# One more pair by seven products in every down quad of a SwiGLU layer, and split row tiles ahead of two phases

## The chip, the cores and the metric

The kernel runs on one core of a Trainium2 chip. The metric is the device time of one execution in microseconds (us); three runs of the kernel before gave a median of 1873.14 us (1871.94 to 1873.9). Engines are named as the profile names them: PE (TensorE, matmuls), PEld (its weight loads), DVE (VectorE), ACT (ScalarE), POOL (GpSimd), SP (SyncE, which issues the DMAs).

## The reference

One decoder layer on 256 tokens of width 2048, in float32. Only the two feed-forward blocks and what lies next to them matter here:

```python
x = x + 0.5 * swiglu(rms_norm(x, g1), w_gate1, w_up1, w_down1)       # FFN1, inner width 5632
h = rms_norm(x, g2); p = h @ w_in                                    # mixing: one projection in
x = x + concat(diff_attention(q, k, v), conv_group(value, gate)) @ w_out
x = x + cross_attention(rms_norm(x, g3), rms_norm(mem, gm))          # ends with @ w_o
x = x + 0.5 * swiglu(rms_norm(x, g4), w_gate2, w_up2, w_down2)       # FFN2, inner width 5632

def swiglu(h, w_gate, w_up, w_down):
    return (silu(h @ w_gate) * (h @ w_up)) @ w_down
```

## The kernel before

All weights (365 MB) come in once as float32 through DMAs that SP issues. Every product is made of three matmul passes on split operands: a weight tile `raw` is cast by ACT to `wh` (L145), and DVE subtracts, `wl = raw - wh` (L146); the activations are split likewise into a high and a low half (`xh`, `xl` for the normed input, `hth`, `htl` for FFN's inner values). High by high, high by low and low by high are summed in PSUM.

The feed-forward blocks run in *quads* (`quad`, L199): four accumulators `acc00` to `acc11`, two token halves by two 512-column blocks. A quad goes through its *parts*, each a pair of 128-row weight tiles of both column blocks: one buffer `raw` of 128x4x512, filled by two DMAs of 512 KB. There are three such buffers (`RAWS`) and seven pairs `wh`, `wl` of 128x1024 (`SPLITS`). An *ordinary part* takes two splits of 1024 columns (so two casts and two subtractions) and 24 matmuls of 128x512. A *seven part* forms the block product with seven products in place of eight: DVE makes sums of weight tiles (L241 to L244), three splits of 1024 columns and one of 512 are needed, and PE does 21 matmuls. Three of the seven products go straight to accumulators, four to the extra sums `p1`, `q6` and `q57`, which `combine` (L286) puts together behind the last seven part; `middle` then adds them to where they belong. A seven part needs sums of the activations too (`token_sums`, L296).

FFN's inner width is 11 chunks of 512, taken in groups of 4, 4 and 3. For each chunk there is one *up quad* of eight parts (gate and up), of which parts 1, 3 and 5 are sevens (`S_IN`); FFN1's first chunk has none. Behind a group stand two *down quads* (`n0` = 0 and 2, one for each half of the output columns): a *down pair*. Their parts are the row pairs of the group's chunks, eight or six, in the order `ORDER_DOWN`; an even part whose chunk number is under `S_DOWN` is a seven: three of eight, two of six. At a down quad's end DVE adds the four accumulators to the residual `X` (L482), and `middle` (L472) adds the seven parts' sums to it in five operations (L477). Where the same X is normed next, `after_x` (L400) books the transposes of the result with `later`, due after so many parts.

`proj` (L149) is the simpler loop for mixing and cross attention: row pairs, two splits of 1024 columns, 24 matmuls. Phases follow in this order: FFN1 to about 714 us, mixing with `w_in` and `w_out`, cross attention with `w_o`, FFN2 from 1167 us to the end. At a boundary the buffers' pools change.

A scheduler in the framework puts each engine's instructions into one fixed order beforehand; at run time an engine waits in this order for semaphores, and buffers come free as their readers end.

Of the kernel before, what the change touches and what calls it, by code (L numbers as in the profile page):

```python
# [52 lines left out]
def hybrid_layer(ctx, tc, x, head, xT, mem, memT, pos, convw, bvec, w):  # L53
# [95 lines left out]
    def proj(stats, srcs, evac, acc=None):  # L149
# [10 lines left out]
        for k0 in range(0, nk, per):  # L160
# [11 lines left out]
            ending = evac is not None and k0 + per >= nk  # L172
            for tb in range(2):

                for js in ([[j] for j in range(nj)] if ending else [list(range(nj))]):
                    for k in ks:
                        h, l, i, _ = stats[k]
                        hs = h[:, i, tb * P:(tb + 1) * P]
                        ls = l[:, i, tb * P:(tb + 1) * P]
                        for j in js:  # L180
                            T.matmul(acc[tb][j], hs, wt[k, j][0], start=(fresh and k == 0), stop=False)  # L181
                            T.matmul(acc[tb][j], hs, wt[k, j][1], start=False, stop=False)  # L182
                        for j in js:
# [15 lines left out]
    def quad(parts, srcs, middle, evac, first=False):  # L199
# [6 lines left out]
        acc = [[accp.tile([P, 512], F32, tag=f"acc{tb}{j}", name=f"acc{tb}{j}") for j in range(2)]  # L206
               for tb in range(2)]
        begun = set()
        seven = [i for i, p in enumerate(parts) if p()[4]]
        q = None  # L210
        for n, part in enumerate(parts):
# [177 lines left out]
    class LazyStats:  # L389
        def __init__(self, norm):  # L390
            self.norm = norm

        def __len__(self):
            return KD

        def __getitem__(self, k):
            h, l = self.norm.grp[k // 4] if self.norm.grp[k // 4] else (None, None)
# [11 lines left out]
    def ffn(norm, wg, wu, wd, groups, done):  # L409
        with tc.tile_pool(name="wf", bufs=SPLITS, reuse_waits="tile") as wf, \  # L410
# [8 lines left out]
            for gi, ng in enumerate(groups):  # L419
                hts, hsums, hold = {}, {}, {}  # L420
                s_down = S_DOWN[ng]
                for c in range(c0, c0 + ng):
# [3 lines left out]
                    sevens = () if start else S_IN  # L426
# [10 lines left out]
                    def evac(tb, acc, c=c, rest=rest, end=(c == c0 + ng - 1), pairs=(c - c0 < s_down)):  # L437
# [12 lines left out]
                        def turn():  # L450
# [16 lines left out]

                    quad(norm.parts(order, sevens),
                         [wg[:, c * 512:(c + 1) * 512], wu[:, c * 512:(c + 1) * 512]], middle, evac, first=start)
                final = gi == len(groups) - 1  # L470
                for n0 in (0, 2):
                    def middle(q, n0=n0):  # L472
                        p1, vw = combine(q, fp)
                        for tb, j, t, f in ((0, 0, p1, 0.5), (0, 1, vw[:, 0, :], 0.5), (1, 0, vw[:, 1, :], -0.5),
# [4 lines left out]
                    def evac(tb, acc, n0=n0):  # L479
                        for j in range(2):  # L480
# [97 lines left out]
    def constants_b():  # L578
# [64 lines left out]
    ffn(n1, w["ffn1_w_gate"], w["ffn1_w_up"], w["ffn1_w_down"], (4, 4, 3),  # L643
        lambda tb, n: after_x(n2, tb, n))
# [41 lines left out]
    w_in, w_out, w_kv = w["w_in"], w["w_out"], w["xattn_w_kv"]  # L686
# [5 lines left out]
    with tc.tile_pool(name="mix", bufs=1, reuse_waits="tile") as mp:  # L692
# [8 lines left out]
        for c in range(2):  # L701
# [12 lines left out]
            proj(n2.stats(), [wcols(w_in, 8 + c), wcols(w_in, 6 + c)], evac)  # L714
# [264 lines left out]
    with tc.tile_pool(name="xa", bufs=1, reuse_waits="tile") as ap:  # L979
# [77 lines left out]
        def add_x2(n0):  # L1057
# [5 lines left out]
            return evac  # L1063
        for n0 in (0, 2):
            proj(xst, [wcols(w["xattn_w_o"], n0), wcols(w["xattn_w_o"], n0 + 1)], add_x2(n0))
# [8 lines left out]
    ffn(n4, w["ffn2_w_gate"], w["ffn2_w_up"], w["ffn2_w_down"], (4, 4, 3), store)  # L1074
# [41 lines left out]
```

## Time and profile before

| | |
|---|---|
| median of three runs | 1873.14 us (1871.94 to 1873.9) |
| profiled execution | 1874.74 us, its span 1871.8 us |
| TensorE clock granted, mean over the span | 0.998 |
| busy: PE, PEld, DVE, ACT | 1852.2, 1524.5, 1676.7, 1090.6 us |
| weights read | 361.09 MB from HBM |

Busy time is the sum of an engine's instructions; matmuls overlap one another, and the ends of matmuls are modelled, so the distance of two starts tells their pace better than a duration. A view by stretch gives each engine's busy time in a window; a window's length less an engine's busy time is that engine's idle time there. A timeline lists instructions by start; in square brackets stands how long the engine had been idle before one, and whose result ended this.

### The profile page before, as it was taken

To read this page: it belongs to the slowest core of one execution; us is meant where nothing else is said; L and a number is where in the kernel's file an instruction comes from. 1 tells how busy PE (TensorE), PEld (TensorE's weight loads), DVE (VectorE), ACT (ScalarE), POOL (GpSimd) and SP (SyncE) were. 2 spreads that over 40 slices of the span, in tenths; PEclk is the share of its full clock that TensorE was granted. 3 is DMA by queue.
4 is the path that set the end of the run, shared out by engine and by line. 5 is a ranking of instruction groups with operands and counts; after the bars stand their busy time and mean duration, and the time that the engine had idled before them with its cause. 6 is when DMAs were issued, how large, how long until landed. Compare 5 with 4: busy or idle time off the path is not lost.

```text
span 1871.8 us, 23348 instructions
## 1 busy us (share of the span) xinstructions
PE 1852.2 (99%) x8365; PEld 1524.5 (81%) x8365; DVE 1676.7 (90%) x2240; ACT 1090.6 (58%) x1470; POOL 21.7 (1%) x29
## 2 busy tenths in 40 slices
PE   9999999999999999999999999999999999999998
PEld 6878888888888887888778887888888888888887
DVE  7899999999999996799997666999999999999998
ACT  7565555565545665554577656665655556555553
POOL 0000000000000000000011000000000000000000
PEclk9999999999999999999999999999999999999999
DMA  9556556656665546766644751556655666546554
GB/s 336 199 193 203 180 176 214 212 187 200 205 222 181 202 158 209 230 206 198 178 134 129 256 182 57 203 180 215 207 191 197 227 212 203 191 157 225 186 201 153
DMA packets 188756, 364.72 MB, mean 195 GB/s; under 512 B 11616, under 2 KB 12128, under 8 KB 188640
## 3 DMA queue, kind: packets, MB, share of 16 engines
q1 hardware_dynamic: 188640, 363.23, 58.6%
q8 instruction: 65, 1.06, 0.2%
q14 instruction: 51, 0.42, 0.1%
HBM read 361.09 MB, written 2.10 MB: 194 GB/s over the span
## 4 chain that ended last, share of the span: by engine, by line
PE 71%; DVE 19%; DMA 3%; issue 3%; ACT 3%; POOL 0%; SPq 0%; DVEq 0%; ACTq 0%
PE acc L277 13%; PE acc L281 13%; PE acc L279 13%; DVE wl L146 8%; DVE y L917 4%; PE acc L182 4%; PE acc L181 4%; PE acc L184 4%; PE acc L196 3%; PE q L196 3%; PE q L197 3%; PE acc L197 3%; PE q L195 3%; PE acc L195 3%; DMA raw<-ffn_w_up 2%
## 5 line engine op out<-in xcount | busy, mean ns | idle before, releaser
L145 ACT CAST wh<-raw 128x1024 fp32r<-128x1024 f32 (+1 forms) x864 | 838.3, 1001 | 664.2 <-DVE raw L241 267.0
L146 DVE TENSOR_TENSOR wl<-raw,wh 128x1024 fp32r<-128x1024 f32 (+1 forms) x864 | 975.9, 1158 | 139.6 <-ACT wh L145 124.2
L277 PE MATMUL acc<-wh,xh_f 128*128 128x512 f32 x904 | 352.7, 393 | 6.5 <-ACT wh L145 3.6
L279 PE MATMUL acc<-wl,xh_f 128*128 128x512 f32 x904 | 351.6, 391 | 0.0
L281 PE MATMUL acc<-wh,xl_f 128*128 128x512 f32 x904 | 294.4, 390 | 0.0
L277 PEld LDWEIGHTS acc<-wh,xh_f 128*128 128x128 f32 x904 | 169.7, 188 | 45.9 <-ACT wh L145 6.0
L279 PEld LDWEIGHTS acc<-wl,xh_f 128*128 128x128 f32 x904 | 170.1, 188 | 36.5 <-DVE wl L146 2.0
L281 PEld LDWEIGHTS acc<-wh,xl_f 128*128 128x128 f32 x904 | 170.0, 188 | 35.5
L277 PE MATMUL acc<-wh,hth 128*128 128x512 f32 x448 | 174.7, 392 | 0.7 <-DVE vw L442 0.4
L279 PE MATMUL acc<-wl,hth 128*128 128x512 f32 x448 | 174.5, 390 | 0.0
L281 PE MATMUL acc<-wh,htl 128*128 128x512 f32 x448 | 147.9, 390 | 0.0
L181 PE MATMUL acc<-wh,xh_mix 128*128 128x512 f32 x320 | 125.6, 394 | 1.8 <-ACT wh L145 1.8
L182 PE MATMUL acc<-wl,xh_mix 128*128 128x512 f32 x320 | 125.3, 392 | 0.5 <-DVE wl L146 0.5
L241 DVE TENSOR_TENSOR raw<-raw 128x1024 f32<-128x1024 f32 x95 | 115.5, 1216 | 0.0
L196 PE MATMUL q<-wl,sh 128*128 128x512 f32 x285 | 110.9, 389 | 0.0
L197 PE MATMUL q<-wh,sl 128*128 128x512 f32 x285 | 110.9, 389 | 0.0
L195 PE MATMUL q<-wh,sh 128*128 128x512 f32 x285 | 110.9, 389 | 0.0
L184 PE MATMUL acc<-wh,xl_mix 128*128 128x512 f32 x320 | 102.9, 391 | 0.0
L917 DVE SCALAR_TENSOR_TENSOR y<-uT,cw,y 128x256 f32<-128x256 f32 x240 | 100.4, 470 | 0.1
L277 PEld LDWEIGHTS acc<-wh,hth 128*128 128x128 f32 x448 | 84.1, 188 | 19.7 <-DVE vw L442 1.3
L281 PEld LDWEIGHTS acc<-wh,htl 128*128 128x128 f32 x448 | 84.1, 188 | 17.6
L279 PEld LDWEIGHTS acc<-wl,hth 128*128 128x128 f32 x448 | 84.2, 188 | 16.9
(299 smaller groups left out, 2502.7 us busy)
## 6 DMA issues: line engine op xcount, KB each, us to landing
raw<-ffn_w_down SPq DMA_DIRECT2D x176, 512.0 KB, 4.8
raw<-ffn_w_gate SPq DMA_DIRECT2D x175, 512.0 KB, 4.0
raw<-ffn_w_up SPq DMA_DIRECT2D x175, 512.0 KB, 5.2
raw<-w_in SPq DMA_DIRECT2D x80, 512.0 KB, 4.4
raw<-w_out SPq DMA_DIRECT2D x32, 512.0 KB, 4.8
raw<-xattn_w_kv SPq DMA_DIRECT2D x16, 512.0 KB, 3.9
raw<-xattn_w_q SPq DMA_DIRECT2D x8, 512.0 KB, 4.3
raw<-xattn_w_o SPq DMA_DIRECT2D x8, 512.0 KB, 3.8
```

Of the source, the lines that this page charges most:

```text
L145: last[:] = [S.copy(out=wh, in_=raw), V.tensor_tensor(out=wl, in0=raw, in1=wh.bitcast(F32), op=ALU.subtract)]
L146: V.tensor_tensor(out=wl, in0=raw, in1=wh.bitcast(F32), op=ALU.subtract)]
L181: T.matmul(acc[tb][j], hs, wt[k, j][0], start=(fresh and k == 0), stop=False)
L182: T.matmul(acc[tb][j], hs, wt[k, j][1], start=False, stop=False)
L184: T.matmul(acc[tb][j], ls, wt[k, j][0], start=False, stop=(ending and k == nk - 1))
L195: T.matmul(acc, hs, w[0], start=start, stop=False)
L196: T.matmul(acc, hs, w[1], start=False, stop=False)
L197: T.matmul(acc, ls, w[0], start=False, stop=stop)
L277: T.matmul(acc[tb][j], hs, wt[b][j][0], start=f"{tb}{j}" not in begun, stop=False)
L279: T.matmul(acc[tb][j], hs, wt[b][j][1], start=False, stop=False)
L281: T.matmul(acc[tb][j], ls, wt[b][j][0], start=False, stop=(ending and b == 1))
L917: V.scalar_tensor_tensor(out=yc, in0=u[:, j:j + 256], scalar=cw[:, j * 8 + ct:j * 8 + ct + 1], in1=yc, op0=ALU.mult, op1=ALU.add)
```

## The change

1. `S_DOWN` becomes 4 and 3 in place of 3 and 2: every down quad has one more seven part, so twelve in the kernel. Its parts are in a new order, in which the last seven parts stand one behind another (2, 4, 6 after 1, 3, 0, 5; or 0, 2, 4 after 1, 3). The last chunk of a group now needs token sums as well.
2. In the down pairs but those that end a block, `middle` only forms `ys`, and four additions to X (five before) stand behind the accumulators' own.
3. A new class `Lead`: the first row pair of mixing's `w_in` (columns 8 and 6) is loaded and split in FFN1's tiles, at the start of the ending part of its last down quad, and its 24 matmuls come straight behind that quad. FFN2's first gate and up row pair is treated so behind cross attention's last `proj`.
4. FFN2's first quad has sevens at 1 and 5 (before 1, 3 and 5) and another order of parts; part 0 is the lead. Some transposes of normed X are due one part later.

```diff
-ORDER_1 = (0, 2, 1, 4, 3, 6, 5, 7)
+S_1, ORDER_1 = (1, 5), (0, 2, 3, 1, 4, 5, 6, 7)
-S_DOWN = {4: 3, 3: 2}
-ORDER_DOWN = {4: (1, 3, 0, 5, 2, 6, 4, 7), 3: (1, 3, 0, 4, 2, 5)}
+S_DOWN = {4: 4, 3: 3}
+ORDER_DOWN = {4: (1, 3, 0, 5, 2, 4, 6, 7), 3: (1, 3, 0, 2, 4, 5)}
...
+    class Lead:
+        def __init__(self, stats, srcs):
+            self.stats, self.srcs = stats, srcs
+
+        def split(self, tiles):
+            self.w = []
+            for src, (raw, wh, wl) in zip(self.srcs, tiles):
+                nc.sync.dma_start(out=raw, in_=rows_pair(src, 0))
+                split(raw, wh, wl)
+                self.w.append((wh, wl))
+
+        def multiply(self):
+            acc = [[accp.tile([P, 512], F32, tag=f"acc{tb}{j}", name=f"acc{tb}{j}") for j in range(2)]
+                   for tb in range(2)]
+            for tb in range(2):
+                for k in range(2):
+                    h, l, i, _ = self.stats[k]
+                    hs, ls = [t[:, i, tb * P:(tb + 1) * P] for t in (h, l)]
+                    for j in range(2):
+                        wh, wl = [t[:, k, :] for t in self.w[j]]
+                        T.matmul(acc[tb][j], hs, wh, start=(k == 0), stop=False)
+                        T.matmul(acc[tb][j], hs, wl, start=False, stop=False)
+                    for j in range(2):
+                        T.matmul(acc[tb][j], ls, self.w[j][0][:, k, :], start=False, stop=False)
+            step()
+            return acc
...
-            later((1, 2, 2, 3)[n], lambda: norm.turn(n))
+            later(((1, 2, 3, 3) if norm.wanted else (1, 2, 3, 4) if norm is n2 else (1, 2, 2, 3))[n],
+                  lambda: norm.turn(n))
...
-                    sevens = () if start else S_IN
+                    sevens = () if start else S_1 if c == 0 else S_IN
...
                         p1, vw = combine(q, fp)
+                        if not final:
+                            y = fp.tile([P, 512], F32, tag="y", name="ys", bufs=1)
+                            V.tensor_tensor(out=y, in0=vw[:, 0, :], in1=q["q57"][:, 1, :], op=ALU.add)
+                            rest[:] = [(0, 0, p1, 0.5), (0, 1, vw[:, 0, :], 0.5), (1, 0, vw[:, 1, :], -0.5),
+                                       (1, 1, y, 0.5)]
+                            return
...
                             if final:
                                 done(tb, n0 + j)
+                        if tb:
+                            for b, j, t, f in rest:
+                                xt = X[b][n0 + j]
+                                V.scalar_tensor_tensor(out=xt, in0=t, scalar=f, in1=xt, op0=ALU.mult, op1=ALU.add)
...
+                    def ahead():
+                        raw = ph["raw"].tile([P, 4, 512], F32, tag="raw", name="raw")
+                        follow.split([(raw[:, 2 * j:2 * j + 2, :], *split_tiles()) for j in range(2)])
+
+                    leads = final and n0 == 2 and follow
+                    quad(parts, [wd[:, n * 512:(n + 1) * 512] for n in (n0, n0 + 1)], middle, evac,
+                         ahead=ahead if leads else None)
+                    if leads:
+                        return follow.multiply()
...
         for n0 in (0, 2):
-            proj(xst, [wcols(w["xattn_w_o"], n0), wcols(w["xattn_w_o"], n0 + 1)], add_x2(n0))
+            proj(xst, [wcols(w["xattn_w_o"], n0), wcols(w["xattn_w_o"], n0 + 1)], add_x2(n0),
+                 ahead=n0 == 2 and (lambda: lead.split([weight_tiles() for _ in range(2)])))
+        open_acc = lead.multiply()
```

What the scheduler makes of it, first on DVE where FFN1's first down pair goes from its first to its second quad. The numbers behind names are buffers; `wl_2056` to `wl_2093` are the second quad's first two parts, `acc00_1710` is the first quad's accumulator. Before:

```order
L146 TENSOR_TENSOR wl_2056<-raw_2054,wh_2055 128x1024
L146 TENSOR_TENSOR wl_2058<-raw_2054,wh_2057 128x1024
L477 SCALAR_TENSOR_TENSOR x00_73<-p1s_2000,x00_73 128x512
L146 TENSOR_TENSOR wl_2091<-raw_2089,wh_2090 128x1024
L291 TENSOR_TENSOR us_2002<-q6_1821,p1s_2000 128x512
L146 TENSOR_TENSOR wl_2093<-raw_2089,wh_2092 128x1024
L293 TENSOR_TENSOR vw_2004<-q57_1822,us_2002 128x1024
L482 SCALAR_TENSOR_TENSOR x00_73<-acc00_1710,x00_73 128x512
L477 SCALAR_TENSOR_TENSOR x01_74<-vw_2004,x01_74 128x512
L477 SCALAR_TENSOR_TENSOR x10_77<-vw_2004,x10_77 128x512
L477 SCALAR_TENSOR_TENSOR x11_78<-vw_2004,x11_78 128x512
L482 SCALAR_TENSOR_TENSOR x01_74<-acc01_1711,x01_74 128x512
```

The same place after; `wl_2077` and `wl_2079` are the second quad's first part:

```order
L146 TENSOR_TENSOR wl_2077<-raw_2075,wh_2076 128x1024
L328 TENSOR_TENSOR vw_2024<-q57_1834,us_2022 128x1024
L534 SCALAR_TENSOR_TENSOR x00_73<-acc00_1710,x00_73 128x512
L522 TENSOR_TENSOR ys_2026<-vw_2024,q57_1834 128x512
L534 SCALAR_TENSOR_TENSOR x01_74<-acc01_1711,x01_74 128x512
L534 SCALAR_TENSOR_TENSOR x10_77<-acc10_1712,x10_77 128x512
L534 SCALAR_TENSOR_TENSOR x11_78<-acc11_1713,x11_78 128x512
L541 SCALAR_TENSOR_TENSOR x00_73<-p1s_2020,x00_73 128x512
L541 SCALAR_TENSOR_TENSOR x01_74<-vw_2024,x01_74 128x512
L541 SCALAR_TENSOR_TENSOR x10_77<-vw_2024,x10_77 128x512
L541 SCALAR_TENSOR_TENSOR x11_78<-ys_2026,x11_78 128x512
L146 TENSOR_TENSOR wl_2079<-raw_2075,wh_2078 128x1024
```

Four splits of the second quad stood ahead of the accumulators' updates; now one does, and the second comes behind nine operations on ys and X.

On PE at the same place, after, from the seventh matmul of the second quad's first part on:

```order
L312 MATMUL acc00_2071<-wh_2078,hth_143 128x512
L312 MATMUL acc01_2072<-wh_2078,hth_143 128x512
L312 MATMUL acc10_2073<-wh_2076,hth_143 128x512
L314 MATMUL acc10_2073<-wl_2077,hth_143 128x512
L312 MATMUL acc11_2074<-wh_2076,hth_143 128x512
L314 MATMUL acc11_2074<-wl_2077,hth_143 128x512
L316 MATMUL acc10_2073<-wh_2076,htl_144 128x512
L316 MATMUL acc11_2074<-wh_2076,htl_144 128x512
L312 MATMUL acc10_2073<-wh_2078,hth_143 128x512
L312 MATMUL acc11_2074<-wh_2078,hth_143 128x512
L228 MATMUL p1_2167<-wh_2148,hth_143 128x512
L314 MATMUL acc00_2071<-wl_2079,hth_143 128x512
```

With the six before these rows, 17 matmuls stand ahead of the first that reads `wl_2079`; before, the fifth matmul of the quad read the second split (`wl_2058`).

On DVE at the end of FFN1's last down quad, after (`wl_6109` and `wl_6111` are the lead's, of mixing's first row pair; `x02_75` to `x13_80` are the X tiles that the quad ends in):

```order
L326 TENSOR_TENSOR us_6087<-q6_5976,p1s_6085 128x512
L146 TENSOR_TENSOR wl_6109<-raw_6107,wh_6108 128x1024
L328 TENSOR_TENSOR vw_6089<-q57_5977,us_6087 128x1024
L146 TENSOR_TENSOR wl_6111<-raw_6107,wh_6110 128x1024
L529 SCALAR_TENSOR_TENSOR x03_76<-vw_6089,x03_76 128x512
L529 SCALAR_TENSOR_TENSOR x12_79<-vw_6089,x12_79 128x512
L529 SCALAR_TENSOR_TENSOR x13_80<-vw_6089,x13_80 128x512
L534 SCALAR_TENSOR_TENSOR x02_75<-acc00_5859,x02_75 128x512
```

The lead's two splits, which before came behind the phase's end, stand ahead of the four accumulators' updates.

## Rows read from the trace of the kernel before

**Rows 1.** The page's first part: busy time, share of span, instructions.

```profile
PE 1852.2 (99%) x8365; PEld 1524.5 (81%) x8365; DVE 1676.7 (90%) x2240; ACT 1090.6 (58%) x1470; POOL 21.7 (1%) x29
```

**Rows 2.** By stretch: start:end, length, busy (x instructions), clock, DMA share, GB/s.

```profile
core 0: us, PE busy (x) PEld busy (x) DVE busy (x) ACT busy (x) POOL busy (x), PEclk, DMA share, GB/s
193.40:271.70 78.30, 77.59 (x342) 63.91 (x342) 71.87 (x79) 39.03 (x42) 0.00 (x0) 1.00 0.62 202
447.00:524.30 77.30, 77.30 (x342) 63.88 (x341) 71.01 (x78) 38.74 (x41) 0.00 (x0) 1.00 0.62 204
1347.00:1426.60 79.60, 79.60 (x352) 65.61 (x351) 74.09 (x81) 41.60 (x45) 0.00 (x0) 1.00 0.59 198
1600.00:1679.50 79.50, 79.50 (x352) 65.67 (x351) 73.20 (x81) 40.52 (x44) 0.00 (x0) 1.00 0.61 199
657.60:715.00 57.40, 56.82 (x263) 46.95 (x262) 51.68 (x64) 30.96 (x46) 0.33 (x2) 1.00 0.44 141
1812.80:1868.20 55.40, 54.06 (x238) 44.22 (x237) 48.81 (x56) 23.58 (x25) 0.00 (x0) 1.00 0.48 161
268.30:437.50 169.20, 168.49 (x756) 139.46 (x755) 160.23 (x184) 99.08 (x114) 0.00 (x0) 1.00 0.61 205
713.50:718.50 5.00, 2.05 (x12) 1.09 (x10) 3.65 (x8) 4.53 (x11) 0.70 (x1) 0.94 0.95 314
718.50:722.50 4.00, 4.00 (x12) 3.20 (x13) 4.00 (x6) 2.98 (x5) 0.00 (x0) 0.64 0.60 156
```

**Rows 3.** Groups by line and shape, DVE: busy us, mean ns, idle before.

```profile
L146 DVE TENSOR_TENSOR wl<-raw,wh 128x1024 fp32r<-128x1024 f32 x765 | 914.1, 1219 | 138.0 <-ACT wh L145 122.8
L146 DVE TENSOR_TENSOR wl<-raw,wh 128x512 fp32r<-128x512 f32 x99 | 67.6, 683 | 1.6 <-ACT wh L145 1.4
L243 DVE TENSOR_TENSOR raw<-raw 128x512 f32<-128x512 f32 x95 | 65.5, 690 | 2.7
L306 DVE TENSOR_TENSOR sl<-sraw,sh 128x512 fp32r<-128x512 f32 x22 | 15.0, 684 | 2.1 <-ACT sh L305 1.8
```

**Rows 4.** Timeline of PE in a down quad: start, duration (us); parts' first matmuls.

```profile
196.16 0.39 PE L195 MATMUL acc<-wh,hth 128*128 128x512 f32 x1
...
200.92 0.39 PE L277 MATMUL acc<-wh,hth 128*128 128x512 f32 x1
...
206.36 0.39 PE L195 MATMUL acc<-wh,hth 128*128 128x512 f32 x1
```

**Rows 5.** Timeline of DVE and PE behind the first down pair.

```profile
274.29 2.50 DVE L146 TENSOR_TENSOR wl<-raw,wh 128x1024 fp32r<-128x1024 f32 x2
274.74 0.39 PE L195 MATMUL acc<-wh,xh_f 128*128 128x512 f32 x1
...
280.72 1.22 DVE L241 TENSOR_TENSOR raw<-raw 128x1024 f32<-128x1024 f32 x1
...
283.31 6.51 DVE L146 TENSOR_TENSOR wl<-raw,wh 128x1024 fp32r<-128x1024 f32 x6
289.74 1.22 DVE L241 TENSOR_TENSOR raw<-raw 128x1024 f32<-128x1024 f32 x1
```

**Rows 6.** Timeline of DVE: token sums of a chunk.

```profile
183.32 0.28 DVE L299 TENSOR_TENSOR sraw<-hold 128x128 f32<-128x128 f32 x1
183.52 0.28 DVE L300 TENSOR_TENSOR sraw<-hold 128x128 f32<-128x128 f32 x1
```

**Rows 7.** Timeline at the end of FFN1 and the start of mixing.

```profile
713.76 1.27 DVE L482 SCALAR_TENSOR_TENSOR x<-acc,x 128x512 f32<-128x512 f32 x2
...
717.22 0.73 PE L181 MATMUL acc<-wh,xh_mix 128*128 128x512 f32 x2 [1.85 <-ACT wh L145]
...
724.50 0.62 PE L184 MATMUL acc<-wh,xl_mix 128*128 128x512 f32 x2
```

**Rows 8.** Timeline of PE: FFN2's first matmuls, and its fourth up quad's.

```profile
1168.02 1.21 PE L277 MATMUL acc<-wh,xh_f 128*128 128x512 f32 x4 [1.07 <-ACT wh L145]
...
1297.67 0.50 PE L277 MATMUL acc<-wh,xh_f 128*128 128x512 f32 x1 [0.98 <-DVE vw L442]
```

**Rows 9.** Timeline: DVE's last two updates of X.

```profile
1866.92 1.27 DVE L482 SCALAR_TENSOR_TENSOR x<-acc,x 128x512 f32<-128x512 f32 x2
```

More of the change, by code (lines that the diff above doesn't have):

```diff
@@ L146, in split, with proj @@
                    V.tensor_tensor(out=wl, in0=raw, in1=wh.bitcast(F32), op=ALU.subtract)]
-    def proj(stats, srcs, evac, acc=None):
+    def proj(stats, srcs, evac, acc=None, ahead=None):
         nj = len(srcs)
@@ L172, in proj @@
             ending = evac is not None and k0 + per >= nk
+            if ending and ahead:
+                ahead()
             for tb in range(2):
@@ L197, in passes, with quad @@
         T.matmul(acc, ls, w[0], start=False, stop=stop)
[L199 to L208, printed above, removed]
+    def quad(parts, srcs, middle, evac, first=False, acc=None, ahead=None):
+        begun = {"00", "01", "10", "11"} if acc else set()
+        acc = acc or [[accp.tile([P, 512], F32, tag=f"acc{tb}{j}", name=f"acc{tb}{j}") for j in range(2)]
+                      for tb in range(2)]
         seven = [i for i, p in enumerate(parts) if p()[4]]
@@ L270, in quad @@
                 ending = n == len(parts) - 1
+                if ending and ahead:
+                    ahead()
                 wt = [[ev0, ev1], [od0, od1]]
@@ L389, in hybrid_layer, with __init__, after @@
     class LazyStats:
-        def __init__(self, norm):
-            self.norm = norm
+        def __init__(self, norm, first=0):
+            self.norm, self.first = norm, first
+        def after(self, k):
+            return LazyStats(self.norm, k)
         def __len__(self):
-            return KD
+            return KD - self.first
         def __getitem__(self, k):
+            k += self.first
             h, l = self.norm.grp[k // 4] if self.norm.grp[k // 4] else (None, None)
@@ L642, in hybrid_layer @@
     n2 = Norm(G_MIX, "mix")
-    ffn(n1, w["ffn1_w_gate"], w["ffn1_w_up"], w["ffn1_w_down"], (4, 4, 3),
-        lambda tb, n: after_x(n2, tb, n))
+    w_in = w["w_in"]
+    open_acc = ffn(n1, w["ffn1_w_gate"], w["ffn1_w_up"], w["ffn1_w_down"], (4, 4, 3),
+                   lambda tb, n: after_x(n2, tb, n),
+                   follow=Lead(n2.stats(), [w_in[:, c * 512:(c + 1) * 512] for c in (8, 6)]))
     mids = ctx.enter_context(ExitStack())
@@ L713, in evac @@
                 later(2, turn)
-            proj(n2.stats(), [wcols(w_in, 8 + c), wcols(w_in, 6 + c)], evac)
+            ks = n2.stats()
+            if c == 0:
+                proj(ks.after(2), [wcols(w_in, 8), wcols(w_in, 6)], evac, acc=open_acc)
+            else:
+                proj(ks, [wcols(w_in, 8 + c), wcols(w_in, 6 + c)], evac)
         later(5, lambda: behind_last(lambda: preload(AF.Exp)))
```

21 lines of the change are left out of this document (13 added, 8 removed).

## The prediction

> **What bounds the kernel now.** I read the page's first part, then one view of busy time by stretch, then timelines of single places. PE is busy 99% of the span, DVE 90% [rows 1]. The shares hide stages, so the stretches matter: four down pairs behind groups of four chunks (start and end of each: 193.4 to 271.7, 447.0 to 524.3, 1347.0 to 1426.6, 1600.0 to 1679.5), two behind groups of three (657.6 to 715.0, 1812.8 to 1868.2) and the four up quads of FFN1's second group (268.3 to 437.5) [rows 2]. The reader is to see two things. PE has almost no gap in a down pair (77.59 of 78.30, 77.30 of 77.30), so PE sets the pace today. And DVE has little left: idle is length less busy, 6.4, 6.3, 5.5 and 6.3 us in the four large pairs, 5.7 and 6.6 us in the small ones. In the up quads it is 9.0 of 169.2 us. So a change that takes work from PE and gives it to DVE is decided by DVE's idle time, pair by pair.
>
> **What one more seven costs and saves.** On PE a seven part takes 200.92 − 196.16 = 4.76 us and an ordinary part 206.36 − 200.92 = 5.44 us [rows 4]: 21 and 24 matmuls at 0.2267 us, so 0.68 us less for each converted part.
>
> On DVE the starts of two like adds at 280.72 and 289.74 stand 9.02 us apart, with one seven and one ordinary part between [rows 5]. The six splits there (five full, one half) take 6.51 us; the half is 0.68 alone [rows 3], so a full one comes every (6.51 − 0.68)/5 = 1.17 us. An ordinary part is two of them, 2.33; the seven is 9.02 − 2.33 = 6.69. Converting costs DVE 4.36 us. To it come token sums: a group's last chunk, which had none, now needs them. Their small subtractions start 0.20 apart [rows 6], four of them and the 0.68 us subtraction of the casts' copies [rows 3] make 1.48. A pair of down quads gets 2 × 4.36 + 1.48 = 10.2 us of DVE work and loses 1.36 us of PE work. ACT gets three full casts and some copies more, beside 39 us busy of 78 [rows 2]: nothing. DMA carries the same bytes at a share of 0.62 or less in these stretches: nothing.
>
> Here a rule of the Trainium skill can be weighed. The trace shows starts of full splits 1.17 us apart though each lasts 1.219 us [rows 3, 5]. "VectorE: DVE Perf Modes", section "The DRAIN you can't avoid", says that the next operation does not start until the pipe is empty. By that, every operation would cost its whole duration: a conversion 6.94 − 2.44 = 4.50, twelve of them 1.7 us more than in my sum. The trace does not agree for this stream, and I keep 4.36.
>
> **The large pairs.** All of a pair's idle DVE time can at best be used, so DVE arrives late by 10.2 less the idle time: 3.8, 3.9, 4.7, 3.9 us. Against it stands a slack: behind a pair, the first seven part of the next up quad starts on PE at 274.74 and needs its third split after nine matmuls, at 274.74 + 2.04 = 276.78. That split starts at 274.29 and is ready at 274.29 + 1.22 = 275.51 [rows 5], 1.27 us early. I take the same for the other three. PE waits for what is over: 2.5 + 2.6 + 3.4 + 2.6 = **+11.1 us**. PE's saved 1.36 us per pair is not to be taken off again: a PE that has less to do waits longer for the same split. Nothing is carried from one pair into the next, since in an up quad PE takes 10.20 us for a seven and an ordinary part and DVE 9.02, so DVE regains its lead, and each pair pays anew. Where the waits stand the order tells: seven parts 2, 4 and 6 now follow one another at the end of a down quad, and each takes DVE 6.69 against PE's 4.76. The seven pairs of split buffers hold three and a half ordinary parts, so the stock runs out there. At the join of the two quads PE has 17 matmuls (3.85 us) before the first one that needs the second split of the new quad, which DVE now does behind nine operations on X and ys; before, two full parts were split by then. Deferring the four X additions is worth nothing by itself (same operations, behind the accumulators' updates); if it freed the accumulators earlier, PE's gap there is 0.7 us per pair at most (78.30 − 77.59).
>
> Bounds for these four pairs: if none of the idle time were usable they would cost 4 × (10.2 − 1.27) = 36 us; if all lateness sank into the buffers, PE's four times 1.36 would come back, −5.4 us. I stay with +11.1, since DVE's waits for casts in the trace are short and its idle time otherwise comes from full buffers.
>
> **FFN1's last pair and the start of mixing.** Before, DVE's last two updates of X end at 713.76 + 1.27 = 715.03, PE then waits 1.85 us for a cast, and the first 24 matmuls of mixing end at 724.50 + 0.62 = 725.1 [rows 7]. In 713.5 to 722.5 PE loses 5.0 − 2.05 = 2.95 us idle and, at a granted clock of 0.64 for 4.0 us, 1.4 us more [rows 2]. The lead row removes the wait: its two loads go out on SP behind the last down part's instead of behind the phase, its casts on ACT and its two splits on DVE stand ahead of the updates. But those updates are late now: by 10.2 − 5.7 = 4.5 us and the two splits' 2.3, so they end at 721.8. Updates come 0.6 apart (two take 1.27), so the first of four accumulators is free at 721.8 − 1.8 = 720.0; the 24 lead matmuls find the next ones free in time and end at 725.4, and the eight transposes, which stood ahead of them (at most 2.05 − 0.73 = 1.3 us, since the two matmuls at 717.22 lie in that stretch too; I take 0.9), follow: 726.3 against 725.1, **+1.2 us**. Bounds: −3.4 if DVE is not late (the 4.4 us lost fall to 1.0), +4 if the clock falls as before and the next row pair is late too.
>
> **FFN2's start.** The wait of 1.07 us for the first cast goes, since the lead covers it. That of 0.98 us for vw at the start of the fourth up quad, where DVE is still behind from the phase's start, goes too [rows 8]: the first quad has one seven less, 4.36 us less for DVE, and two ordinary parts stand behind its last seven. For PE the missing seven is +0.68. **−1.4 us**; between −2.5 and +0.7.
>
> **FFN2's last pair.** It ends in DVE's updates of X, the last two at 1866.92 [rows 9], and nothing gives slack behind it: 10.2 − 6.6 = **+3.6 us**; between −1.4 and +6.
>
> **Sum.** 11.1 + 1.2 − 1.4 + 3.6 = +14.5. The profiled execution took 1874.74 us (span 1871.8), so 1889.2; the runs' median of 1873.14 is 1.6 lower, so **1888 us**.
>
> **Rivals.** *PE keeps the pace* (faster). The buffers and better order absorb everything: that happens where DVE's arrears at the end of a pair stay under the 1.27 us of slack. For it speaks PE's 99%, and that DVE is 195 us idle over the whole span [rows 1]; against it, that this idle time lies mostly elsewhere and only 5.5 to 6.6 us of it in each pair. Price: eleven net sevens −7.5, boundary −3.4, FFN2's start −2.1 (the waits alone; its seven is in the eleven), together −13.0: 1860 us.
> *Half is absorbed.* DVE gets about half of the lateness back from waits that I did not resolve, for instance of the deferred X additions: between the two, 1874 us, no change.
> *Worse* (slower still). A quarter of DVE's 36.8 us of idle time in the six pairs cannot be used, because it is a wait for a cast: ACT's wh ends most of the idle before the full splits (122.8 of 138.0 us [rows 3]). That is +9.2, and if conversions cost 4.50, +1.7: 1899 us. It decides from the point where the longer runs of sevens make ACT's casts and DVE's splits wait for each other in the seven buffers.
> That the change does not do what it says is no rival: the order shows twelve more seven parts and both lead rows.
>
> **How the numbers follow.** My forecast (own range 1881 to 1895) 0.55; PE keeps the pace 0.19; half 0.14; worse 0.12. About 0.2%, 3.7 us, is what a measurement of this kernel can tell from no change. Faster by more: 0.19 and a third of the half case, 0.24. Same: 0.08, from the half case. Slower: 0.68. The range 1866 to 1898 holds my case, the half case, half of the worse and a sixth of the fast one, about 0.8.
>
> **What would show it.** After the change PE must show gaps that end on DVE's wl: at the start of the second down quad, at the third split of a seven in the run 2, 4, 6, and in the first seven behind a pair, 2.5 to 3.4 us in each large pair; DVE's idle time in the pairs must fall to about 1 us. If PE shows no such gaps and DVE still idles 3 us or more in a pair, the fast rival is right and the step from lateness to waiting is wrong. If DVE idles and PE waits, ACT or the buffers are the cause. At mixing's start I expect no wait for a cast but one for the accumulator, released by an X update; at 1168 no gap.

## Result and the profile after

The changed kernel took 1896.55 us (median of four runs, 1894.89 to 1900.49) against 1872.56 us for the kernel before: a ratio of 1.013, 95% interval 1.0113 to 1.0148. That is 24.0 us slower, where 15 were forecast: 1896.55 us lies just above the forecast's own range (1881 to 1895) and inside the wide one (1866 to 1898). The profiled execution took 1900.49 us, the longest of the four, span 1898.7 us, 26.9 us more than the span before; the stretches below account for these 26.9. Busy times, where [rows 1] stood:

```profile
PE 1855.8 (98%) x8332; PEld 1517.9 (80%) x8332; DVE 1729.3 (91%) x2325; ACT 1110.8 (59%) x1510; POOL 20.4 (1%) x29
```

DVE has 52.6 us more work and PE 33 matmuls fewer. PE's busy time rose all the same. It was not taken apart, but matmuls behind a wait are shown longer (0.50 us where 0.39 is usual, in the rows below), and so are those at half the clock. Where time went is seen from the starts of each stage's first matmul on PE. The third column is the changed kernel with the old table of sevens (experiment 1). All in us:

| stretch | before | after | old sevens |
|---|---|---|---|
| start to the first down pair | 183.55 | 184.74 | 181.62 |
| FFN1, first large pair and the up quads behind | 254.39 | 258.03 | 253.56 |
| FFN1, second | 210.25 | 214.44 | 210.12 |
| FFN1's last pair, mixing, to `w_o` | 492.27 | 498.95 | 487.47 |
| `w_o` and FFN2's first up quads | 199.33 | 196.63 | 196.63 |
| FFN2, first large pair and the up quads behind | 253.05 | 257.05 | 252.49 |
| FFN2, second | 210.25 | 214.82 | 210.12 |
| FFN2's last pair to the end | 68.75 | 74.07 | 68.67 |

The first stretch varied between 181.2 and 184.7 us among the kernels run here and is left out of the reasoning: it took 181.7 us or less where the granted clock held, and 182.9 or more where it fell to 0.50 for 3.41 us near 15 us, as in both kernels' profiled executions. The large pairs gave +3.6, +4.2, +4.0 and +4.6, 16.4 together; FFN1's last pair with mixing +6.7, FFN2's start −2.7, FFN2's end +5.3.

The view by stretch, of the same places as [rows 2] (down pairs without their first two parts, then the four up quads, then FFN1's end):

```profile
core 0: us, PE busy (x) PEld busy (x) DVE busy (x) ACT busy (x) POOL busy (x), PEclk, DMA share, GB/s
194.60:274.40 79.80, 78.03 (x340) 63.31 (x340) 77.53 (x91) 41.75 (x49) 0.00 (x0) 1.00 0.56 185
452.60:530.60 78.00, 76.37 (x334) 62.10 (x333) 75.62 (x88) 41.22 (x47) 0.00 (x0) 1.00 0.58 188
1360.00:1439.60 79.60, 77.67 (x340) 63.20 (x339) 76.99 (x89) 43.53 (x51) 0.00 (x0) 1.00 0.57 185
1616.00:1698.50 82.50, 80.72 (x353) 65.48 (x352) 79.67 (x92) 44.56 (x52) 0.00 (x0) 1.00 0.55 179
666.50:730.40 63.90, 58.13 (x254) 45.43 (x252) 61.84 (x78) 35.84 (x52) 0.33 (x2) 1.00 0.44 140
1834.50:1894.50 60.00, 55.50 (x232) 44.05 (x230) 57.31 (x70) 26.56 (x31) 0.00 (x0) 0.97 0.45 146
271.00:442.50 171.50, 169.34 (x756) 139.58 (x756) 163.74 (x188) 99.54 (x116) 0.00 (x0) 1.00 0.62 209
...
728.90:739.45 10.55, 8.32 (x35) 6.53 (x33) 7.56 (x13) 4.94 (x11) 0.70 (x1) 0.84 0.54 175
```

DVE's idle time in the pairs fell from 5.5 to 6.6 us to 2.3, 2.4, 2.6, 2.8, 2.1 and 2.7: not to about 1. PE now has gaps of 1.6 to 5.8 us in each, where it had 1.3 or less. In FFN2's last pair the clock's mean is 0.97. There, behind waits of 0.47, 0.69 and 0.92 us at the join of the two quads, the granted clock fell to 0.50, that is to 1.2 GHz, for 3.41 us; before, it was 1.00 in this pair:

```profile
1861.90:1865.30 3.40, 3.40 (x10) 2.63 (x9) 3.40 (x4) 0.00 (x0) 0.00 (x0) 0.50 0.65 187
```

PE's waits, by what they wait for (us in total, times, longest), the first of the list after:

```profile
PE acc L228 <- ACT wh L145: 10.1, 12, 1.0
PE acc L314 <- DVE wl L146: 4.8, 5, 1.1
PE p L228 <- ACT wh L145: 4.5, 5, 1.1
```

L228 is the first pass of each of a seven part's products. Behind FFN1's first down pair and in it, timeline of PE; then of DVE in the run of sevens 2, 4, 6 of its first quad; then ACT's casts that end three of these waits:

```profile
232.81 0.50 PE L228 MATMUL p<-wh,hth 128*128 128x512 f32 x1 [1.07 <-ACT wh L145]
...
262.94 0.50 PE L228 MATMUL acc<-wh,hth 128*128 128x512 f32 x1 [0.59 <-ACT wh L145]
...
276.17 0.73 PE L314 MATMUL acc<-wl,xh_f 128*128 128x512 f32 x2 [1.12 <-DVE wl L146]
281.65 0.50 PE L228 MATMUL acc<-wh,xh_f 128*128 128x512 f32 x1 [0.95 <-ACT wh L145]
```

```profile
210.99 0.68 DVE L277 TENSOR_TENSOR raw<-raw 128x512 f32<-128x512 f32 x1
212.86 2.96 DVE L146 TENSOR_TENSOR wl<-raw,wh 128x1024 fp32r<-128x1024 f32 x3 [1.20 <-ACT wh L145]
215.75 1.22 DVE L274 TENSOR_TENSOR raw<-raw 128x1024 f32<-128x1024 f32 x1
```

```profile
211.78 2.52 ACT L145 CAST wh<-raw 128x1024 fp32r<-128x1024 f32 x3 [2.02 <-DVE raw L277]
...
231.19 1.56 ACT L145 CAST wh<-raw 128x1024 fp32r<-128x1024 f32 x2 [2.72 <-DMA raw<-ffn_w_down]
...
280.55 2.00 ACT L145 CAST wh<-raw 128x1024 fp32r<-128x1024 f32 x2 [0.40 <-DVE raw L277]
```

Three of PE's four waits are at places named beforehand: the join of the two down quads (232.81), the third seven of the run in the second quad (262.94) and the first seven behind the pair (281.65); the one at the first part behind the pair (276.17) was not named. Only that one ends on DVE's `wl`, as forecast of all of them; the others end on a cast. One step back it is DVE again: at 281.65 the cast is of a tile that DVE had only just summed (L277). At this join the cast is of an unsummed tile, behind a wait for its load (231.19). But DVE's split for the matmul behind ended within 0.3 us of that cast, here and at the joins of the other three large pairs, so either would have held PE.

DVE's one large idle stretch, 1.20 us at 212.86, stands inside the run, ahead of part 4's last split, with PE on time. The cast that it waits for was not held by a full buffer: ACT itself had waited, for 2.02 us, for the sum that DVE had just ended at 210.99 + 0.68. DVE sums, ACT casts the sum, DVE splits it, and DVE's fixed order puts nothing between. Each of the six down pairs has one such wait, of 1.17 to 1.20 us.

At the two boundaries and the end, where [rows 7 to 9] stood:

```profile
731.52 0.47 PE L216 MATMUL acc<-wh,xh_mix 128*128 128x512 f32 x1 [2.23 <-DVE x L534]
...
1181.59 0.39 PE L216 MATMUL acc<-wh,xh_f 128*128 128x512 f32 x1
...
1893.78 1.28 DVE L534 SCALAR_TENSOR_TENSOR x<-acc,x 128x512 f32<-128x512 f32 x2
```

Mixing's first matmul no longer waits for a cast but for an X update on DVE, 2.23 us; FFN2's first comes 0.23 us behind the one before it, without a wait.

### The profile page after: what moved, and what is told of

It is laid out like the page before. It is cut to its first block, busy times and chain, and to the rows that moved or that the text cites. A ratio compares the mean times of both kernels' runs of the same rounds, so it can differ in the third digit from the quotient of the medians.

```text
span 1898.7 us, 23374 instructions
## 1 busy us (share of the span) xinstructions
PE 1855.8 (98%) x8332; PEld 1517.9 (80%) x8332; DVE 1729.3 (91%) x2325; ACT 1110.8 (59%) x1510; POOL 20.4 (1%) x29
## 4 chain that ended last, share of the span: by engine, by line
PE 57%; DVE 27%; DMA 6%; issue 5%; ACT 4%; SPq 0%; POOL 0%; ACTq 0%; DVEq 0%
DVE wl L146 11%; PE acc L316 9%; PE acc L314 9%; PE acc L312 9%; DVE y L987 4%; PE acc L183 4%; PE acc L186 4%; PE acc L184 4%; ACT wh L145 3%; DMA raw<-ffn_w_down 2%; DVE raw L274 2%; PE acc L228 2%; PE q L229 2%; PE q L230 2%; PE acc L229 2%
## 5 line engine op out<-in xcount | busy, mean ns | idle before, releaser
L145 ACT CAST wh<-raw 128x1024 fp32r<-128x1024 f32 (+1 forms) x886 | 851.7, 997 | 658.8 <-DVE raw L274 270.8
L146 DVE TENSOR_TENSOR wl<-raw,wh 128x1024 fp32r<-128x1024 f32 (+1 forms) x886 | 996.0, 1154 | 119.4 <-ACT wh L145 105.7
L312 PE MATMUL acc<-wh,hth 128*128 128x512 f32 x352 | 135.1, 395 | 3.4 <-DVE x L534 1.4
L314 PE MATMUL acc<-wl,hth 128*128 128x512 f32 x352 | 135.3, 393 | 0.4 <-DVE wl L146 0.4
L274 DVE TENSOR_TENSOR raw<-raw 128x1024 f32<-128x1024 f32 x106 | 129.2, 1219 | 0.1
L228 PE MATMUL q<-wh,sh 128*128 128x512 f32 x318 | 124.7, 392 | 1.3 <-ACT wh L145 0.8
L229 PE MATMUL q<-wl,sh 128*128 128x512 f32 x318 | 124.1, 390 | 0.1
L316 PE MATMUL acc<-wh,htl 128*128 128x512 f32 x352 | 116.4, 392 | 0.0
L312 PEld LDWEIGHTS acc<-wh,hth 128*128 128x128 f32 x352 | 66.3, 189 | 19.7 <-DVE x L534 2.9
L314 PEld LDWEIGHTS acc<-wl,hth 128*128 128x128 f32 x352 | 66.4, 189 | 16.2 <-DVE wl L146 2.6
L316 PEld LDWEIGHTS acc<-wh,htl 128*128 128x128 f32 x352 | 66.4, 189 | 13.7
```

Of the source, the lines that this page charges most:

```text
L145: last[:] = [S.copy(out=wh, in_=raw), V.tensor_tensor(out=wl, in0=raw, in1=wh.bitcast(F32), op=ALU.subtract)]
L146: V.tensor_tensor(out=wl, in0=raw, in1=wh.bitcast(F32), op=ALU.subtract)]
L228: T.matmul(acc, hs, w[0], start=start, stop=False)
L229: T.matmul(acc, hs, w[1], start=False, stop=False)
L274: V.tensor_tensor(out=raw[:, 1:3, :], in0=raw[:, 1:3, :], in1=raw[:, 2:4, :], op=ALU.add)
L312: T.matmul(acc[tb][j], hs, wt[b][j][0], start=f"{tb}{j}" not in begun, stop=False)
```

## Experiments

Times are medians; ratios are against the kernel before on the same chip.

**1. The old sevens, all else changed.**

```diff
-S_DOWN = {4: 4, 3: 3}
-ORDER_DOWN = {4: (1, 3, 0, 5, 2, 4, 6, 7), 3: (1, 3, 0, 2, 4, 5)}
+S_DOWN = {4: 3, 3: 2}
+ORDER_DOWN = {4: (1, 3, 0, 5, 2, 6, 4, 7), 3: (1, 3, 0, 4, 2, 5)}
```

> The changed kernel with the old table of sevens (three of eight, two of six, old order); lead rows, deferred additions and FFN2's first quad stay as changed. Theory (DVE arrears in the down pairs, 26.9 us of span lost there less what the leads give): the loss goes and the leads' gain stays, 2.7 us at FFN2's start and about 1 at mixing's: 1868 to 1870 us. Rival (the leads or the deferred additions cost time themselves): 1873 us or more.

1864.1 us, ratio 0.9958 (0.9943 to 0.9972), and once more, with more rounds:

> The changed kernel with the old table of sevens once more, for comparison on the same chip and with more rounds: 1863 to 1866 us by its first runs.

1864.6 us, ratio 0.9957 (0.9944 to 0.9969). So the sevens cost 32 us, and the rest of the change gives 8, more than the theory's 3 to 4. By the table, 4.8 of these come from FFN1's end and mixing's start and 2.7 from FFN2's start. Some 1.7 of the 4.8 are the clock: before, it was at 0.50 for 3.41 us from 717.93 on; with the old sevens it was 1.00 from 711.50 to 723.50 (second run). With DVE on time the lead runs straight behind the last down part, 0.22 us after its last matmul (second run):

```profile
711.46 0.39 PE L316 MATMUL acc<-wh,htl 128*128 128x512 f32 x1
711.68 0.39 PE L216 MATMUL acc<-wh,xh_mix 128*128 128x512 f32 x1
```

This version beats both kernels and is the best of those tried.

**2. The sevens alone, on the kernel before.**

```diff
-S_DOWN = {4: 3, 3: 2}
-ORDER_DOWN = {4: (1, 3, 0, 5, 2, 6, 4, 7), 3: (1, 3, 0, 4, 2, 5)}
+S_DOWN = {4: 4, 3: 3}
+ORDER_DOWN = {4: (1, 3, 0, 5, 2, 4, 6, 7), 3: (1, 3, 0, 2, 4, 5)}
...
-                                                                  a == 0 and i // 2 < s_down and hsums[c])
+                                                                  a == 0 and i // 2 < s_down and hsums.get(c, True))
```

> The kernel before with only the new table of sevens (one more in each down quad, new order); no lead, no deferral, old first quad of FFN2. Theory (DVE arrears): all of the loss is here, 1896.5 plus the leads' gain of about 3.5: 1899 to 1902 us. Rival (a good part of the loss comes from the lead's two splits ahead of the X updates at FFN1's end, where 6.5 us were lost): 1890 us or less.

1906.5 us, ratio 1.018 (1.0163 to 1.0197): 34 us for the sevens alone. The rival falls. The size was missed here (over the theory's 1902) and in experiment 1 (under its 1868), since the rest of the change gives 8 to 10 us, not 3.5. Of the 10, some 5 are the clock: from the first down pair to 1895 us it was at 0.50 for 17.1 us in this kernel's profiled execution and for 6.8 us in the changed kernel's.

**3. Two ways to take about 5 us of DVE work from each pair.** First the added seven's three sums, in its own chain:

```diff
-                V.tensor_tensor(out=raw[:, 1:3, :], in0=raw[:, 1:3, :], in1=raw[:, 2:4, :], op=ALU.add)
...
-                V.tensor_tensor(out=raw[:, 3, :], in0=raw[:, 3, :], in1=raw[:, 1, :], op=ALU.add)
-                V.tensor_tensor(out=raw[:, 0, :], in0=raw[:, 0, :], in1=raw[:, 3, :], op=ALU.add)
+                if n not in bare:
+                    V.tensor_tensor(out=raw[:, 1:3, :], in0=raw[:, 1:3, :], in1=raw[:, 2:4, :], op=ALU.add)
+                    V.tensor_tensor(out=raw[:, 3, :], in0=raw[:, 3, :], in1=raw[:, 1, :], op=ALU.add)
+                    V.tensor_tensor(out=raw[:, 0, :], in0=raw[:, 0, :], in1=raw[:, 3, :], op=ALU.add)
...
+                         ahead=ahead if leads else None, bare=(ORDER_DOWN[ng].index(2 * s_down - 2),))
```

> The changed kernel without the three sums of weight tiles in the one added seven of each down quad (its products then take unsummed tiles: that part of the result is left out). DVE has 2.58 us less per down quad, 5.2 per pair; PE's and ACT's work is the same. Theory (DVE arrears): 10.2 - 5.2 = 5.0 us added per pair, under the idle time of 5.5 to 6.6 that there was, so arrears all but vanish: 1860 to 1865 us. Rival (the casts or PE's own order set the end): 1890 us or more.

1866.5 us, ratio 0.9968 (0.9957 to 0.9979), just over the theory's 1865. Then additions to X, which no product of the pair waits for:

```diff
+                            if tb == 0 and j == 0:
...
-                            for b, j, t, f in rest:
+                            for b, j, t, f in ():
```

> The changed kernel with the four deferred additions of the sevens' sums to X left out in each down quad (in a block's last pair four of five; that part of the result is left out). DVE has 2.4 us less per quad, 4.8 per pair, and none of it in a seven's own chain of sum, cast, product. Theory (DVE's total work in the pair decides): the same recovery as without the sums but for 0.4 us a pair, 1862 to 1867 us. Rival (the chain sum - cast - product in the run of three sevens decides, where PE waits for ACT's wh): little change, 1890 us or more.

1865.2 us, ratio 0.9962 (0.9947 to 0.9977). Both recover 30 us, the one inside the chain of sum, cast and product and the other outside it, about as much as they take from DVE (six pairs of 5.2 and 4.8 us). So it is the amount of DVE's work that costs PE its time, not that chain: in the second the waits of 1.2 us for the cast of a sum still stand (1.19 us at 209.30), and PE does not feel them. There, the first pair (181.18 to 265.29) and the up quads behind:

```profile
181.18:265.29 84.11, 83.60 (x370) 68.19 (x369) 81.96 (x98) 47.98 (x57) 0.00 (x0) 1.00 0.54 180
265.29:434.15 168.86, 168.86 (x758) 139.80 (x756) 161.41 (x184) 99.28 (x115) 0.00 (x0) 1.00 0.63 212
```

With the same sevens PE loses nothing in the up quads (168.86 of 168.86; after the change 169.34 of 171.50).

**4. The order of parts, and the stock of splits.** The same work with the sevens spread:

```diff
-ORDER_DOWN = {4: (1, 3, 0, 5, 2, 4, 6, 7), 3: (1, 3, 0, 2, 4, 5)}
+ORDER_DOWN = {4: (1, 0, 3, 2, 5, 4, 6, 7), 3: (1, 0, 3, 2, 4, 5)}
```

> The changed kernel with the down parts in another order: sevens spread among the ordinary parts, 1, 0, 3, 2, 5, 4, 6, 7 (groups of four) and 1, 0, 3, 2, 4, 5 (groups of three); the same parts, sums and products. In the changed kernel's first pair DVE idles 1.19 us once ahead of the run 2, 4, 6, with all split buffers full, and 0.12 us in each seven; so theory (idle time early in a quad can't be banked beyond the stock): spreading makes some 1 us per down quad usable, 1884 to 1892 us. Rival (only DVE's total in the pair counts): 1895 to 1899 us.

1889.5 us, ratio 1.0098 (1.0081 to 1.0115): 7 us less, the theory's number but not for its reason. The wait of 1.2 us, which it expected to become usable, still stands in each of the six pairs, and it was no wait for split buffers (above). In the first:

```profile
200.32 2.36 DVE L146 TENSOR_TENSOR wl<-raw,wh 128x1024 fp32r<-128x1024 f32 x2 [1.18 <-ACT wh L145]
```

By the stretches 4.4 us of the gain lie in the large pairs and 2.1 in FFN2's last pair, where the granted clock did not fall here. Why the order helps stays open. And with a smaller stock:

```diff
-RAWS, SPLITS, H_BUFS = 3, 7, 4
+RAWS, SPLITS, H_BUFS = 3, 6, 4
```

> The changed kernel with six pairs of split buffers in place of seven. Theory (a seven needs four of them, and what DVE can do ahead of a run of sevens is limited by this stock): one full split less ahead, 1.17 us, in each of 22 quads at most and in each of 12 down quads at least: 1908 to 1922 us. Rival (DVE's total decides and the stock does not): 1895 to 1900 us.

1903.2 us, ratio 1.0165 (1.0151 to 1.0179): 6.7 us more than with seven, under the theory's 1908 and over the rival's 1900, so neither number held. Of the excess 2.7 us stand in `w_o` and FFN2's first up quads, and 0.1 to 1.5 us in each down pair but FFN1's last, which with mixing is 0.4 us shorter. Order and stock each matter, by about 7 us with the same work.

**5. The deferral.**

```diff
-                        if not final:
+                        if False:
```

> The changed kernel with the sevens' sums added to X at once in every down quad, as before the change (five additions instead of ys and four behind the accumulators). The same number of DVE operations. Theory (DVE's total decides, the deferral is worth nothing by itself): 1894 to 1899 us. Rival (deferral frees the accumulators or p1 for PE earlier and was worth a part of the 10 us by which the changed kernel beats the one with the sevens alone): 1900 to 1904 us.

1899.5 us, ratio 1.0151 (1.0136 to 1.0166), between the theory's range and the rival's. The interval overlaps the changed kernel's (1.0113 to 1.0148): by the ratios the deferral is worth 4 us, and anything from nothing to 8 fits. The profiled executions show nothing: from the first down pair to the end they take 1714.0 us both.

**6. One seven more in one quad of a pair**, groups of four only, sevens spread there:

```diff
-S_DOWN = {4: 4, 3: 3}
-ORDER_DOWN = {4: (1, 3, 0, 5, 2, 4, 6, 7), 3: (1, 3, 0, 2, 4, 5)}
+S_DOWN = {4: 4, 3: 2}
+ORDER_DOWN = {4: (1, 3, 0, 5, 2, 6, 4, 7), 3: (1, 3, 0, 4, 2, 5)}
+ORDER_EXTRA, EXTRA = (1, 0, 3, 2, 5, 4, 6, 7), 2
...
+                    extra = n0 == EXTRA and ng == 4
+                    parts = [lambda c=c0 + i // 2, a=i % 2, i=i, m=s_down - (ng == 4 and not extra): (*hts[c], 2 * a, c * 4 + 2 * a,
+                                                                  a == 0 and i // 2 < m and hsums.get(c, True))
+                             for i in (ORDER_EXTRA if extra else ORDER_DOWN[ng])]
```

> The version with the old sevens plus one more seven in the second down quad only, in groups of four only, its parts in the spread order 1, 0, 3, 2, 5, 4, 6, 7 (four sevens more in the kernel). Theory (a pair pays for DVE work beyond its usable idle time and 1.27 us of slack): 4.36 + 1.48 = 5.84 us against 6.4 to 6.9 of idle less about 1.5 unusable, late by some 0.9, under the slack, so PE's 0.68 comes back: 2 to 3 us under the old sevens' 1864.1, 1861 to 1863. Rival (added DVE work always costs, or the fixed gaps in a seven eat more): 1864 to 1870 us.

1870.7 us, ratio 0.9989 (0.998 to 0.9998): just over the rival's 1870. With `EXTRA` at 0 instead:

> The same with the extra seven in the first down quad of a pair, so that a whole quad follows in which DVE can regain its lead. Theory: PE waits inside the first quad by up to 1 us, but the pair's end is as before: 1861 to 1865 us, within 2 us of the run with the extra seven in the second quad. Rival (the stock of splits at the first quad's end is what counts, and the token sums of the last chunk come just then): 1866 us or more.

1868.7 us, ratio 0.9979 (0.997 to 0.9988), in the rival's range. Both are slower than the old sevens' 1864.6, by 6.0 and 4.1 us: the theory's reckoning by whole pairs failed. The extra seven in the second quad shows why. The first pair's first and second quad, and the up quads behind:

```profile
183.25:225.50 42.25, 41.84 (x188) 34.37 (x188) 39.90 (x52) 24.13 (x30) 0.00 (x0) 1.00 0.56 185
225.50:267.30 41.80, 41.80 (x186) 34.59 (x185) 41.29 (x47) 22.57 (x25) 0.00 (x0) 1.00 0.55 182
267.30:437.84 170.54, 169.28 (x757) 139.76 (x756) 163.04 (x188) 99.43 (x115) 0.00 (x0) 1.00 0.62 209
```

and PE in the first seven behind (this kernel's lines are numbered one higher, so L229 is L228 above):

```profile
275.28 0.49 PE L229 MATMUL q<-wh,sh 128*128 128x512 f32 x1 [0.31 <-ACT wh L146]
276.74 0.50 PE L229 MATMUL acc<-wh,xh_f 128*128 128x512 f32 x1 [0.96 <-ACT wh L146]
```

DVE idles 2.35 us in the first quad (42.25 − 39.90), with PE on time, and 0.51 us in the second (41.80 − 41.29); then PE waits. The largest of the first quad's idle stretches, 0.87 us, is one of full buffers: DVE waits for a cast, and the cast for a split buffer that PE frees:

```profile
215.20 1.05 ACT L146 CAST wh<-raw 128x1024 fp32r<-128x1024 f32 x1 [1.24 <-PE acc L317]
```

```profile
216.28 3.96 DVE L147 TENSOR_TENSOR wl<-raw,wh 128x1024 fp32r<-128x1024 f32 x3 [0.87 <-ACT wh L146]
```

What DVE leaves idle so in the first quad, the second can't have. Casts that PE released end 1.5 of the 2.35 us, and one that waited for its load 0.52.

**7. POOL in place of DVE.** The added seven's three sums on POOL:

```diff
-                V.tensor_tensor(out=raw[:, 1:3, :], in0=raw[:, 1:3, :], in1=raw[:, 2:4, :], op=ALU.add)
...
+                E = G if n in other else V
+                E.tensor_tensor(out=raw[:, 1:3, :], in0=raw[:, 1:3, :], in1=raw[:, 2:4, :], op=ALU.add)
+                E.tensor_tensor(out=raw[:, 3, :], in0=raw[:, 3, :], in1=raw[:, 1, :], op=ALU.add)
+                E.tensor_tensor(out=raw[:, 0, :], in0=raw[:, 0, :], in1=raw[:, 3, :], op=ALU.add)
...
+                         ahead=ahead if leads else None, other=(ORDER_DOWN[ng].index(2 * s_down - 2),))
```

> The changed kernel with the three sums of weight tiles of each down quad's added seven on POOL in place of DVE. Theory (DVE's total decides; POOL is idle): near the run without those sums, 1866.5, up to 1875 us. Rival (the sums' chain to the cast counts, which grows with each sum's time on POOL, in the run of three sevens): 1885 us or more.

1939.8 us, ratio 1.0364 (1.0348 to 1.0381): slower by 43 us than with these sums on DVE. The three take 2.77 + 1.30 + 2.14 us in a row, and DVE, behind them in its fixed order, waits for the casts:

```profile
213.76 2.77 POOL L274 TENSOR_TENSOR raw<-raw 128x1024 f32<-128x1024 f32 x1 [169.15 <-DVE wl L146]
216.61 1.30 POOL L275 TENSOR_TENSOR raw<-raw 128x512 f32<-128x512 f32 x1
217.99 2.14 POOL L276 TENSOR_TENSOR raw<-raw 128x512 f32<-128x512 f32 x1
```

```profile
217.66 1.33 DVE L146 TENSOR_TENSOR wl<-raw,wh 128x1024 fp32r<-128x1024 f32 x1 [3.37 <-ACT wh L145]
221.24 4.63 DVE L146 TENSOR_TENSOR wl<-raw,wh 128x1024 fp32r<-128x1024 f32 x4 [2.25 <-ACT wh L145]
```

And the deferred additions on POOL, with one more seven in groups of four alone:

```diff
-S_DOWN = {4: 4, 3: 3}
-ORDER_DOWN = {4: (1, 3, 0, 5, 2, 4, 6, 7), 3: (1, 3, 0, 2, 4, 5)}
+S_DOWN = {4: 4, 3: 2}
+ORDER_DOWN = {4: (1, 3, 0, 5, 2, 4, 6, 7), 3: (1, 3, 0, 4, 2, 5)}
...
-                                V.scalar_tensor_tensor(out=xt, in0=t, scalar=f, in1=xt, op0=ALU.mult, op1=ALU.add)
+                                G.tensor_scalar(out=t, in0=t, scalar1=f, scalar2=None, op0=ALU.mult)
+                                G.tensor_tensor(out=xt, in0=xt, in1=t, op=ALU.add)
```

> A version meant to be best: one more seven in the down quads of groups of four only (groups of three as before), leads kept, and the deferred additions to X on POOL (halved there, then added), which takes 2.4 us of DVE work from each of those quads. Theory: the pairs as without the additions, 0.6 to 0.9 us shorter each than with the old sevens (which gave 1864.1): 1860 to 1864 us. Rival (POOL's accesses slow DVE, or late additions hold buffers that the next quad's combination needs): 1868 us or more.

1904.0 us, ratio 1.0175 (1.016 to 1.019): the rival. DVE in the first pair's join, while POOL works (222.32 to 236.72):

```profile
225.52 1.88 DVE L534 SCALAR_TENSOR_TENSOR x<-acc,x 128x512 f32<-128x512 f32 x3
...
227.31 8.25 DVE L146 TENSOR_TENSOR wl<-raw,wh 128x1024 fp32r<-128x1024 f32 x5
235.49 2.31 DVE L274 TENSOR_TENSOR raw<-raw 128x1024 f32<-128x1024 f32 x1
```

Four full splits and a half one take 8.25 us, where four at 1.17 and one at 0.68 are 5.4, and a sum 2.31 in place of 1.22. The updates of X that read an accumulator keep their 0.6 apart.

## Why the forecast was right, and where it was too small

**The mechanism held.** The forecast was that DVE comes late in every down pair and PE waits for it. The old sevens take the loss away (1), the sevens alone make it (2), and taking some 5 us of DVE's work from each pair takes it away wherever that work stood (3). The rival in which PE keeps the pace stands where DVE is relieved: 1865 to 1867 us.

**The step that failed is "All of a pair's idle DVE time can at best be used", taken as if all of it were.** The large pairs came to +16.4 in place of +11.1, and 2.3 to 2.8 us of each pair's idle time stayed unused. Which part was usable shows when each wait of DVE for a cast is followed back to what that cast had waited for. Before, 4.4 to 5.4 us of the 5.5 to 6.4 in each large pair were full buffers, as the forecast had said: the cast waited until PE had freed a split buffer, as here:

```profile
205.25 1.05 ACT L145 CAST wh<-raw 128x1024 fp32r<-128x1024 f32 x1 [1.23 <-PE acc L281]
```

```profile
206.33 3.19 DVE L146 TENSOR_TENSOR wl<-raw,wh 128x1024 fp32r<-128x1024 f32 x3 [0.87 <-ACT wh L145]
```

After, 0.07 to 0.14 us of this kind are left: this part was used. What is left over is of another kind: the 1.2 us in which DVE waits for the cast of its own sum, and short gaps, most of them between a seven's dependent sums, casts and splits (the longest, 0.34 us, is a wait for a load). The third rival named a quarter of the idle time as unusable, as waits for a cast, and 1899 us. Its size was nearer (some 40% stayed unused), and for the 1.2 us its cause was right, though not by the way that it named, since the buffers were not full there. Where DVE has time to spare, such a wait costs PE nothing (3).

The +11.1 came as near as it did in part by luck. Over these four pairs with their up quads, DVE's busy time rose by 34.3 us, where the forecast had 40.8 of work (its price of a seven holds the short gaps too; the rest of this difference was not taken apart), and its idle time fell by 17.9 us, where the forecast had 24.5 and 5.1 of slack. Both terms were too large, and the errors partly cancel.

Experiment 6 shows that idle time with full buffers can't be kept for later. That a smaller stock costs 7 us fits this; a larger one was not tried.

**FFN1's end and mixing's start**: +6.7 in place of +1.2. The lead row is worth more than the bound given (−4.8 with DVE on time, −3.4 in the text), but the arrears eat it: from the changed to the old sevens this stretch has 11.5 us. I had the first accumulator free at 720.0, which is 729.0 with the stage's start 9.0 us later; PE got it at 731.52. Behind this the granted clock is 0.84 over 728.90 to 739.45, some 10.55 × 0.16 = 1.7 us. The forecast had the 24 lead matmuls at the full clock, so it missed these 1.7 us; against the kernel before they are no loss, since its clock fell at the same place, and with the old sevens it did not.

**FFN2's start**: −2.7, a little beyond the bound of −2.5 and the forecast of −1.4; both waits, of 1.07 and 0.98 us, are gone. What gave the rest stays open. **FFN2's last pair**: +5.3 in place of +3.6, with 2.7 us of idle time left there too. The half clock at 1861.90 costs PE some 1.7 us there, a term that the forecast did not have; how much of it reaches the end, which DVE's updates set, is not shown. **The deferral** at nothing: none shows in the profiled executions, and the medians leave it open. **ACT and DMA** at nothing: ACT is busy 59% of the span. A load does stand behind the cast at the join (231.19), but DVE's split there was as late.

## What to carry to other kernels

When work goes from a full engine to one that is nearly full, count the second engine's free time stretch by stretch, and for each idle stretch ask what the instruction that ended it had itself waited for. Idle time from full buffers can be used, within what the buffers hold. Idle time in a chain that runs through another engine and back is not filled while the order stays fixed, and new work can bring more of it, here 1.2 us per pair. A seven more saves PE 0.68 us and costs DVE 4.36, and even one in a pair with over 6 us of idle DVE time did not pay. And try parts of a change that serve different ends apart: here one part was worth −8 us and the other +32.

## What was not expected of the hardware

POOL, idle 99% of the time, was no help. Its sums of 128x512 took 1.29 and 2.14 us on average where DVE's take 0.69, and DVE's operations with both inputs in SBUF grew beside it, while those that read an accumulator did not (experiment 7). In the kernel with additions on POOL, DVE was busier in the first pair (183.08 to 271.27) than after the change (83.96 us in 184.74 to 271.04), though eight operations of 0.68 us had left it:

```profile
183.08:271.27 88.19, 84.95 (x368) 67.93 (x369) 86.09 (x98) 47.35 (x57) 18.36 (x11) 1.00 0.52 171
```

```profile
184.74:271.04 86.30, 84.12 (x368) 68.08 (x369) 83.96 (x101) 47.62 (x57) 0.00 (x0) 1.00 0.53 175
```

The Trainium skill, "GPSIMD Engine Reference", section "Architecture", says that this engine's one read and one write port into SBUF are shared with DVE, and section "Engine selection" puts its two-input elementwise operations at about half VectorE's speed. The trace shows 2.3 times as long for 128x1024, and 1.9 and 3.1 times for 128x512, so about the half in two of three; with the first it fits, but no run here tells a port from another cause.
